# Splitting the projection's weight tiles by halves, with precedence for those of the values

## The chip, the cores and the metric

The kernel runs on one core of one Trainium2 chip. The metric is the device time of one execution in microseconds (us). The engines are named as in the profile: PE (TensorE, matrix products; PEld are its weight loads), ACT (ScalarE), DVE (VectorE), POOL (GpSimd) and SP (SyncE, which issues nearly all DMAs).

## The reference

The kernel computes one layer of a decoder for x of 1 x 1024 tokens x 1024, in float32. One input projection feeds two mixers side by side: a gated delta rule of 4 heads (mixer A, in chunks, a recurrence over the sequence) and a dilated window attention of 8 heads (mixer B). An output projection of both, and a gated MLP with a short convolution, follow.

```python
h = rmsnorm(x, norm1_w)
proj = h @ w_in                                   # q, k, v, z, beta, decay of A; q, k, v of B
qkv_a = silu(causal_dwconv(qkv_a, conv_qkv_w))    # A: convolution of 4 taps, then l2norm of q and k
o_a = rmsnorm(gated_delta_rule(qa, ka, va, g, beta), gdn_norm_w) * silu(z)
o_b = dilated_attention(qb, kb, vb)               # windows 128, 512, 2048 with strides 1, 4, 16
x = x + concatenate([o_a, o_b]) @ w_out
h = rmsnorm(x, norm2_w)
u = causal_dwconv(h @ w_up, ffn_conv_w)
x = x + (silu(gate) * up) @ w_down
return rmsnorm(x, final_norm_w)
```

## The kernel before, in words

**Products of split numbers.** [...] Each operand is split into a high part (a copy rounded to the type float32r) and a low part (the rest). `mm3` (line 199) multiplies high by high, high by low and low by high into one PSUM bank of 128 x 512. A weight tile of 128 x 1024 is loaded into a buffer wst (`raw_weight`, line 209), then split by `split` (line 205): ACT copies wst to whi, and DVE subtracts whi from wst into wlo. Each of wst, whi and wlo has a ring of two buffers. `weight` (line 214) does the split of one tile in two instructions, one on ACT and one on DVE, over all 1024 columns. `wk` (line 232) is `weight` for the output projection; `wk_by_halves` (line 222) does one tile there in two halves of 512 columns, with the urgent engines described below.

**The projections.** `dense` (line 491) goes through the columns in the order of DENSE (line 44): the last key tile, the values of mixer B in two groups (V 0 and V 1), q and v of mixer A by heads, q, k and v of mixer B by pairs ("a"), z. `take` (line 509) gives the tile that is due, splits the next one and loads the one after that. So a split is issued one tile ahead of its use.

- A V group (`values_by_token`, line 518) has four tokens' blocks as four banks of PSUM (two of the tag asc, two of ch) and four weight tiles j = 0 to 3 of in_wv. A tile holds two blocks of the contraction (kk = 0 and 1) of 512 columns each: for each block, each bank gets one mm3, 24 matrix products a tile. The first product of a bank in a group waits until the bank was emptied. After the group, ACT scales the four banks into vx (line 533, four evictions), and SP stores them by twos (line 535).
- Another tile (m-tile) holds eight blocks of 128 columns, and gives two banks of eight mm3 each, 48 products. Of its banks `scaled` (line 438) makes xr or aqkv on DVE. For keys, q and v of mixer A `conv_silu` (line 454) follows: a scaled copy on ACT, three steps kT<-xr,gcw,kT on DVE, then for keys a tanh (xr<-kT) on ACT and kT<-xr,kT on DVE.

**What else runs beside them.** `kprep` (line 595) prepares a head's keys: it loads rows of the decay into dec and, behind the key's last step, copies its ends to gel (DVE), takes eight exponentials dec<-dec,ngc and eg and ge (ACT), transposes the keys on PE and evicts them as ktok (ACT) with sums of squares sq; DVE makes bp, ke and um of the products of keys. Then come the triangular solve (DVE, some of it on small slices), the chain of the recurrent state over the chunks (ct, wke, r, w, vtok: short steps that alternate between PE, DVE and ACT), and the attention, whose scores sm are evicted with their maximum by DVE, exponentiated by ACT, transposed by PE and copied back as pt and pb by ACT and DVE.

**What sets the order.** PE's order is fixed when the kernel is built: streams of work (the generators above) run against a model of times, `Weave` (line 48), which asks for the `need` of tiles and gives each matrix product a place (`mm`, line 191, stamps it). The wrappers `Engine` (line 123) account ACT, DVE, POOL and SP in the model too, by a fixed part and a part per column. On ACT, DVE and SP the framework's scheduler orders the instructions afterwards by its own priorities: those of the plain wrappers `ac` and `ve` by their place in the program, those of the wrappers `ua` and `uv` (lines 153 and 154) 400 places (URGENT) earlier. Each engine works strictly in its order and waits there for what it needs.

A helper records all instructions under its own line: L141 and L143 in the profile are the ordinary and the urgent calls of the wrappers, L192 the products, L196 the transposes. Tiles are named by out<-in.

Of the kernel before, what the change touches and what calls it, by code (L numbers as in the profile page):

```python
# [7 lines left out]
F32 = mybir.dt.float32  # L8
F32R = mybir.dt.float32r
AF = mybir.ActivationFunctionType  # L10
OP = mybir.AluOpType
# [135 lines left out]
def hybrid_layer(tc, I, out):  # L147
    nc = tc.nc
    wv = Weave()
    ve = Engine(wv, nc.vector, "vector", 0.07, 0.00105)  # L150
    ac = Engine(wv, nc.scalar, "scalar", 0.12, 0.00085)

    uv = Engine(wv, nc.vector, "vector", 0.07, 0.00105, first=tc.high_priority)
    ua = Engine(wv, nc.scalar, "scalar", 0.12, 0.00085, first=tc.high_priority)
# [11 lines left out]
    def tile_(pool, shape, dt, name, tag, bufs):  # L166
        return wv.slot(pool.tile(list(shape), dt, name=name, tag=tag, bufs=bufs), tag, bufs)
# [3 lines left out]
    def A(name, tag, dt=F32, shape=(P, 1024)):  # L171
        if tag in TURNS:
            i = turns[tag] = turns.get(tag, -1) + 1
            tag = TURNS[tag][i % len(TURNS[tag])]
        return tile_(lp, shape, dt, name, tag, SLOTS[tag])
# [23 lines left out]
    def mm3(dst, lhs, rhs, first, last, **kw):  # L199
        us = 0.2135 * rhs[0].shape[-1] / 512  # L200
        mm(dst, lhs[0], rhs[0], us, first, False, **kw)
        mm(dst, lhs[0], rhs[1], us, False, False, **kw)
        mm(dst, lhs[1], rhs[0], us, False, last, **kw)

    def split(src, hi, lo):
        ac.activation(hi, src, AF.Copy)
        return ve.tensor_tensor(lo, src, hi.bitcast(F32), op=OP.subtract)

    def raw_weight(src, n=1024):
        st = tile_(wp, [P, n], F32, "wst", "wst", 2)  # L210
        sy.dma_start(st, src)
        return st

    def weight(src, n=1024, st=None):
        if st is None:
            st = raw_weight(src, n)
        hi = tile_(wp, [P, n], F32R, "whi", "whi", 2)
        lo = tile_(wp, [P, n], F32R, "wlo", "wlo", 2)
        split(st, hi, lo)
        return hi, lo  # L220

    def wk_by_halves(src):
# [34 lines left out]
    def bank(tag, name="ps"):  # L257
        return tile_(pp_, (P, 512), F32, name, tag, 2)
# [7 lines left out]
    def half(i):  # L266
        return slice(i * 512, i * 512 + 512)
# [170 lines left out]
    def scaled(pair, name, by_class=False, tag="ev", t=None, hs=(0, 1)):  # L438
        if t is None:
            t = A(name, tag)  # L440
        for h in hs:
            sl = half(h)
            if by_class:
                ve.tensor_tensor(t[:, sl].rearrange("p (n c u) -> p n u c", n=4, c=4),
                                        pair[h].rearrange("p (n u c) -> p n u c", n=4, c=4),
                                        rstdB[:, sl].rearrange("p (n u c) -> p n u c", n=4, c=4), op=OP.mult)
            else:
                ve.tensor_tensor(t[:, sl], pair[h], rstdB[:, sl], op=OP.mult)
        return t
# [4 lines left out]
    def conv_silu(xr, j, name, tag):  # L454
        y = A(name, tag)
        ac.activation(y, xr, AF.Copy, scale=gcw[:, j, 3:4])
        for d in (1, 2, 3):
            inst = ve.scalar_tensor_tensor(y[:, d:], xr[:, :S - d], gcw[:, j, 3 - d:4 - d], y[:, d:],
                                           op0=OP.mult, op1=OP.add)
            if j // 4 == 1 and d == 2 and klast:  # L460
                after(inst, klast[-1], "the keys before go first")
        if j // 4 != 1:
            ac.activation(y, y, AF.Silu)
            return y

        th = ac.activation(xr, y, AF.Tanh, scale=0.5)
        klast.append(ve.scalar_tensor_tensor(y, xr, 1.0, y, op0=OP.add, op1=OP.mult))
        kends[j - 4] = th, klast[-1]
        return y

    def silu2(xr, name):
        y = A(name, "ev")
        ac.activation(y, xr, AF.Tanh, scale=0.5)
        ve.scalar_tensor_tensor(y, y, 1.0, xr, op0=OP.add, op1=OP.mult)
        return y
# [8 lines left out]
    def first_keys():  # L484
        xr = [scaled(pst[2 * h:2 * h + 2], "xr", tag=("ev", "ev", "qa")[h]) for h in range(3)]
        for h in range(3):
            T["k", h] = conv_silu(xr[h], 4 + h, "kT", "kT*")
            wv.add(3, kprep(h))
            yield wv.need(T["k", h])

    def dense():

        yield from wv.until("first")
        yield from wv.until("norms")
        wv.add(2, first_keys())

        srcs, tiles = [], 0
        for col in DENSE:
            if col[0] == "V":
                srcs += [I["wv"][j] for j in range(4)]  # L500
            else:
                srcs.append(I["wi"][tiles])
                tiles += 1
        place = [0]
        raw = [raw_weight(srcs[0])]
        nxt = [weight(None, st=raw.pop())]
        raw.append(raw_weight(srcs[1]))

        def take():
            w = nxt.pop()  # L510
            i = place[0] = place[0] + 1
            if i < len(srcs):
                nxt.append(weight(None, st=raw.pop()))
            if i + 1 < len(srcs):
                raw.append(raw_weight(srcs[i + 1]))
            return w

        def values_by_token(g):

            banks = [bank(t) for t in ("asc", "asc", "ch", "ch")]  # L520
            for j in range(4):
                w = [t.rearrange("p (k m) -> p k m", k=2) for t in take()]
                for kk in range(2):
                    k = 2 * j + kk
                    for i, pt in enumerate(banks):
                        c = 4 * g + i
                        yield wv.need(pt, *w)
                        mm3(pt, [t[:, c * P:(c + 1) * P] for t in xs[k]], [t[:, kk, :] for t in w], k == 0, k == KT - 1)
            for i in range(0, 4, 2):
                vx = A("vx", "ev", shape=(P, 2, 512))  # L530
                for e in range(2):
                    c = 4 * g + i + e
                    ac.activation(vx[:, e, :], banks[i + e], AF.Copy, scale=rst[:, c:c + 1])
                c = 4 * g + i
                sy.dma_start(vpark[c * P:(c + 2) * P].rearrange("(e p) d -> p e d", e=2), vx)
            wv.done.add(("V", g))

        for i, col in enumerate(DENSE):
            kind, h = col[:2]
            if kind == "V":  # L540
                yield from values_by_token(h)
                continue
            if kind == "z":
                yield from wv.until(("o", h))
            w = [t.rearrange("p (k m) -> p k m", k=KT) for t in take()]
            pair = []
            for hh in range(2):
                pt = bank("hf")
                yield wv.need(pt, *w)
                for k in range(KT):  # L550
                    mm3(pt, [t[:, k, :] for t in w], [t[:, half(hh)] for t in xs[k]], k == 0, k == KT - 1)
                    yield 0.0

                pair.append(pt)
                if hh == 0:
                    xr = A("aqkv" if kind == "a" else "xr", "go" if kind == "k" else "ev")
                scaled(pair, "xr", kind == "a", t=xr, hs=(hh,))
            if kind == "k":
                T["k", h] = conv_silu(xr, 4 + h, "kT", "kT*")
                wv.add(3, kprep(h))  # L560
            elif kind == "q":
                q = conv_silu(xr, h, "qT", "qa")
                wv.add(4, qprep(h, q))
            elif kind == "v":
                v = conv_silu(xr, 8 + h, "vT", "qa")
                wv.add(4, vprep(h, v))
            elif kind == "z":
                og = gated[h] = A("og", "kT*")
                sy.dma_start(og, mixer[h])
                ve.tensor_tensor(og, og, silu2(xr, "zz"), op=OP.mult)  # L570
            else:
                sy.dma_start(apark[h, col[2]], xr)
                wv.done.add(col)
        wv.done.add("dense")
# [100 lines left out]
    def vprep(h, vT):  # L675
        yield from wv.until(("q", h))
        yield wv.need(vT, slack=SLACK)
        G[h]["vtok"] = yield from tokens(vT, A("vtok", ("dv", "dw")[h % 2]), G[h]["nk"])
        wv.done.add(("v", h))
# [952 lines left out]
```

## Time and profile before

| | us |
|---|---|
| median of three runs (lowest, highest) | 1207.66 (1207.51, 1208.27) |
| the profiled execution, its own time | 1208.24 |
| its span, first to last instruction | 1206.4 |
| PE busy | 1193.4 |
| DVE busy | 947.6 |
| ACT busy | 574.7 |
| POOL busy | 48.9 |

The clock granted to PE was 0.998 of full speed. A row of a timeline below has the start (us from the span's start), the length in us, engine, line, operation, out<-in, the shape of one instruction and xcount where neighbours of one kind are put together; in brackets stands the engine's idle time before the row and what ended it. Such a row's length for several instructions is that of all of them. Matmul ends are modelled, so the pitch of PE is read from starts. What an engine issues without being waited for costs nothing while PE is busy; a wait in PE's rows costs its length.

### The profile page before, as it was taken

The page shows a single profiled execution, that of the slowest core. Times are in us where ns is not written, and L with a number is a line of the kernel's source. Part 1 is how long each engine was busy: PE and PEld are TensorE (multiplying, and loading weights), DVE is VectorE, ACT ScalarE, POOL GpSimd, SP SyncE. Part 2 cuts the span into 40 slices and gives each one's busy share as a digit, 9 for nine tenths or more (in the row PEclk, how much of TensorE's full clock was granted, in tenths as well). Part 3 has the DMA queues.
Part 4 walks back from the last instruction along what each step waited for, and adds up shares of the span by engine and source line. Part 5 has one row for each costly group of instructions (what it writes and reads, how often), then busy time and mean ns, then how long its engine had stood idle before and what let it go on. Part 6 is the DMA issues. An engine that isn't in the chain of part 4 may idle for free.

```text
span 1206.4 us, 18292 instructions
## 1 busy us (share of the span) xinstructions
PE 1193.4 (99%) x7068; PEld 983.7 (82%) x7068; DVE 947.6 (79%) x1462; ACT 574.7 (48%) x1126; POOL 48.9 (4%) x46
## 2 busy tenths in 40 slices
PE   9999999999999999999999999999999999999997
PEld 7878888888777778888888888888888888888886
DVE  7684965666477686767988988889898889999875
ACT  7384344356344452655545445444454454444441
POOL 0211010003100000000000000000000000000000
PEclk9999999999999999999999999999999999999999
DMA  7425253435624213544213132231322298546513
GB/s 233 109 74 160 82 128 112 146 123 151 227 98 128 82 36 107 175 136 150 75 66 105 54 104 85 72 105 53 105 69 89 93 367 307 180 161 226 165 54 140
DMA packets 85798, 154.80 MB, mean 128 GB/s; under 512 B 21168, under 2 KB 36304, under 8 KB 85712
## 3 DMA queue, kind: packets, MB, share of 16 engines
q1 hardware_dynamic: 85136, 153.12, 39.5%
q8 instruction: 55, 0.90, 0.3%
q10 hardware_dynamic: 576, 0.52, 0.1%
q14 instruction: 31, 0.25, 0.1%
HBM read 117.68 MB, written 35.93 MB: 127 GB/s over the span
## 4 chain that ended last, share of the span: by engine, by line
PE 94%; DVE 3%; issue 1%; ACT 1%; POOLq 0%; POOL 0%; DVEq 0%; ACTq 0%
PE ps L192 43%; PE pa L192 20%; PE dw L192 17%; PE pc L192 10%; PE ps L196 3%; DVE kT L141 1%; PE warm L192 1%; DVE wlo L141 1%; DVE xr L141 0%; DVE x1h L141 0%; PE pd L192 0%; DVE sm L143 0%; DVE qT L141 0%; ACT dec L141 0%; ACT sq L143 0%
## 5 line engine op out<-in xcount | busy, mean ns | idle before, releaser
L192 PE MATMUL dw<-pr 128*128 128x512 f32 (+1 forms) x984 | 211.3, 376 | 0.0
L192 PEld LDWEIGHTS dw<-pr 128*128 128x128 f32 x984 | 176.6, 188 | 33.6
L192 PE MATMUL ps<-xhi,whi 128*128 128x512 f32 x384 | 158.1, 412 | 0.0
L192 PE MATMUL ps<-xhi,wlo 128*128 128x512 f32 x384 | 150.3, 391 | 0.0
L192 PE MATMUL ps<-xlo,whi 128*128 128x512 f32 x384 | 149.9, 390 | 0.0
L192 PE MATMUL pa<-T,pair 128*128 128x512 f32 x528 | 127.1, 389 | 0.0
L192 PEld LDWEIGHTS pa<-T,pair 128*128 128x128 f32 x528 | 99.0, 188 | 20.6
L192 PEld LDWEIGHTS ps<-xhi,wlo 128*128 128x128 f32 x384 | 72.1, 188 | 15.7
L192 PEld LDWEIGHTS ps<-xhi,whi 128*128 128x128 f32 x384 | 72.2, 188 | 14.8 <-issue 1.4
L192 PEld LDWEIGHTS ps<-xlo,whi 128*128 128x128 f32 x384 | 72.4, 189 | 12.0
L141 ACT ACTIVATE u<-pa 128x512 f32<-128x512 f32 x44 | 26.3, 598 | 107.3 <-PE pa L192 107.3
L141 ACT ACTIVATE whi<-wst 128x1024 fp32r<-128x1024 f32 (+2 forms) x41 | 41.9, 1022 | 74.0 <-PE ps L192 64.7
L141 DVE SCALAR_TENSOR_TENSOR y<-xu,fcw,y 128x1023 f32<-128x1023 f32 (+1 forms) x44 | 56.4, 1281 | 22.1 <-ACT y L141 22.0
L143 ACT ACTIVATE sm<-sm,mx 128x128 f32<-128x128 f32 (+7 forms) x64 | 35.4, 555 | 60.0 <-DVE mx L143 60.0
L192 PE MATMUL pa<-B,A 128*128 128x512 f32 x264 | 63.4, 389 | 0.0
L192 PE MATMUL pc<-T,S 128*128 128x512 f32 x264 | 63.4, 389 | 0.0
L192 PE MATMUL pa<-T,S 128*128 128x512 f32 x264 | 63.4, 389 | 0.0
L192 PE MATMUL pc<-B,pair 128*128 128x512 f32 x264 | 63.4, 389 | 0.0
L141 DVE TENSOR_TENSOR wst<-wst 128x512 f32<-128x512 f32 x88 | 60.6, 688 | 0.9
L192 PE MATMUL ps<-B,pair 128*128 128x512 f32 x252 | 60.5, 389 | 0.0
L141 DVE TENSOR_TENSOR wlo<-wst,whi 128x1024 fp32r<-128x1024 f32 (+2 forms) x41 | 48.2, 1175 | 14.9 <-ACT whi L141 14.9
L192 PEld LDWEIGHTS pa<-B,A 128*128 128x128 f32 x264 | 49.5, 188 | 10.3
(244 smaller groups left out, 2349.2 us busy)
## 6 DMA issues: line engine op xcount, KB each, us to landing
wst<-in_wu SPq DMA_DIRECT2D x44, 512.0 KB, 3.7
wd<-in_wd SPq DMA_DIRECT2D x44, 512.0 KB, 4.4
upark<-y SPq DMA_DIRECT2D x22, 512.0 KB, 3.8
wst<-in_wi SPq DMA_DIRECT2D x21, 512.0 KB, 3.7
r<-upark SPq DMA_DIRECT2D x11, 512.0 KB, 7.4
r<-upark SPq DMA_DIRECT2D x22, 256.0 KB, 6.8
wa<-in_wd SPq DMA_DIRECT2D x22, 256.0 KB, 3.1
wst<-in_wv SPq DMA_DIRECT2D x8, 512.0 KB, 3.6
```

What stands on the lines that cost most here:

```text
L141: return getattr(eng, op)(*a, **kw)
L143: return getattr(eng, op)(*a, **kw)
L192: tc.stamp_issue_order_token(nc.tensor.matmul(dst, lhs, rhs, start=start, stop=stop, **kw).ins, TOKEN)
L196: tc.stamp_issue_order_token(nc.tensor.transpose(dst, src, ident if idt is None else idt).ins, TOKEN)
```

## The change

`weight` splits a tile in two halves of 512 columns, each with one copy on ACT and one subtraction on DVE; where `urgent` is given, these go through the wrappers `ua` and `uv`. `take` gives `urgent` for the tiles that are split on its first eight calls: the eight tiles of in_wv. All tiles of 128 x 1024 that go through `weight` are split by halves: 21 of in_wi, 8 of in_wv and 7 of in_wo, 36 tiles, so ACT and DVE have 36 instructions more each. The matrix products, the loads, the buffers and the numbers computed stay the same.

```diff
-    def weight(src, n=1024, st=None):
+    def weight(src, n=1024, st=None, urgent=False):
         if st is None:
             st = raw_weight(src, n)
         hi = tile_(wp, [P, n], F32R, "whi", "whi", 2)
         lo = tile_(wp, [P, n], F32R, "wlo", "wlo", 2)
-        split(st, hi, lo)
+        for sl in (half(0), half(1)):
+            (ua if urgent else ac).activation(hi[:, sl], st[:, sl], AF.Copy)
+            (uv if urgent else ve).tensor_tensor(lo[:, sl], st[:, sl], hi[:, sl].bitcast(F32), op=OP.subtract)
         return hi, lo
...
             w = nxt.pop()
             i = place[0] = place[0] + 1
             if i < len(srcs):
-                nxt.append(weight(None, st=raw.pop()))
+                nxt.append(weight(None, st=raw.pop(), urgent=1 <= i <= 8))
             if i + 1 < len(srcs):
                 raw.append(raw_weight(srcs[i + 1]))
             return w
```

## The prediction

> **What bounds the kernel now.** I read the page first: the span, the busy shares and the chain that ended last.
>
> ```profile
> span 1206.4 us, 18292 instructions
> PE 1193.4 (99%) x7068; PEld 983.7 (82%) x7068; DVE 947.6 (79%) x1462; ACT 574.7 (48%) x1126; POOL 48.9 (4%) x46
> PE 94%; DVE 3%; issue 1%; ACT 1%; POOLq 0%; POOL 0%; DVEq 0%; ACTq 0%
> ```
>
> The matmul engine is busy in 1193.4 of 1206.4 us. No edit of splits takes a matmul away, so all that can be won is PE's idle time, 13.0 us in the whole span, and all that can be lost is new idle time on PE. The waits of PE by releaser say how much of it belongs to weights:
>
> ```profile
> PE ps L192 <- DVE wlo L141: 1.1, 1, 1.1
> PE ps L192 <- ACT whi L141: 0.4, 1, 0.4
> ```
>
> One wait each. The timeline of PE shows where they are, the third tile (j=2) of the first value group:
>
> ```profile
> 73.41 0.39 PE L192 MATMUL ps<-whi,xlo 128*128 128x512 f32 x1
> 74.20 0.51 PE L192 MATMUL ps<-whi,xhi 128*128 128x512 f32 x1 [0.41 <-ACT whi L141]
> 75.83 0.50 PE L192 MATMUL ps<-wlo,xhi 128*128 128x512 f32 x1 [1.12 <-DVE wlo L141]
> 76.16 0.39 PE L192 MATMUL ps<-whi,xlo 128*128 128x512 f32 x1
> 76.39 0.40 PE L192 MATMUL ps<-whi,xhi 128*128 128x512 f32 x1
> ```
>
> Unhindered products start 0.23 us apart (76.16 to 76.39). Here they start 0.79 and 1.63 apart: 0.56 + 1.40 = 1.96 us is lost to this tile, and this is the whole prize. The timelines of ACT and DVE show why it is late:
>
> ```profile
> 70.54 2.47 ACT L141 ACTIVATE dec<-dec,ngc 128x128 f32<-128x128 f32 x8
> 72.98 0.22 ACT L141 ACTIVATE ge<-gel 128x8 f32<-128x8 f32 x1
> 73.08 1.07 ACT L141 ACTIVATE whi<-wst 128x1024 fp32r<-128x1024 f32 x1
> 70.71 3.92 DVE L141 SCALAR_TENSOR_TENSOR kT<-xr,gcw,kT 128x1023 f32<-128x1023 f32 x3 [0.23 <-ACT kT L141]
> 74.55 1.22 DVE L141 TENSOR_TENSOR wlo<-wst,whi 128x1024 fp32r<-128x1024 f32 x1
> ```
>
> ACT comes to the high part only after eight exponentials of the decay, DVE to the low part only after three steps of a convolution. PE waits for DVE last.
>
> **The change part by part.** *The halves' price.* One tile of the kernel is already split by halves (its rows are L143 here), so the price is in the trace (ACT's timeline, and the tile view with least, median and most):
>
> ```profile
> 495.79 1.15 ACT L143 ACTIVATE whi<-wst 128x512 fp32r<-128x512 f32 x2 [5.41 <-PE ps L192]
> L143 DVE TENSOR_TENSOR wlo<-wst,whi x2: 685/686/686, 496.6 to 497.8; 128x512 fp32r<-128x512 f32 x2
> ```
>
> Two halves on ACT take 1.15 us against 1.07 for the whole tile at 73.08: 0.08 more. On DVE 2 x 0.686 - 1.22 (74.55) = 0.15 more, less the overlap of neighbours (the whole split of 74.55 follows a group that ends at 74.63, 0.08 later): 0.07. With 36 tiles of 128x1024 that is 36 x 0.08 = 2.9 us on ACT and 36 x 0.07 = 2.5 us on DVE. Neither is on the chain; a weight tile is taken one tile ahead, and a tile is 48 products (11 us) long in the m-tiles, 24 (5.5 us) in the values' tiles. I cost this at nothing. It is covered by PE; without that cover it would be 2.5 to 2.9 us.
>
> *The stalled tile.* In the built order of the changed kernel the precedence moves this tile's high halves past one instruction only, ge (0.1 us of issue, 72.98 to 73.08), and its low halves not at all: they still stand behind the three kT steps. So only the halving helps. DVE starts half a at 74.55 and ends it 0.69 later, at 75.24, instead of 75.77. PE gains about 0.5 us (floor 0, if the kT steps end later; ceiling 1.96, had the precedence put the split first).
>
> *The other value tiles, and a new wait.* The precedence does move the splits of the tiles behind. Three moves matter:
>
> ```profile
> 78.14 1.23 DVE L141 SCALAR_TENSOR_TENSOR kT<-xr,kT 128x1024 f32<-128x1024 f32 x1
> 79.48 2.45 ACT L141 ACTIVATE dec<-dec,ngc 128x128 f32<-128x128 f32 x8 [0.43 <-DVE gel L141]
> 80.55 1.12 DVE L141 SCALAR_TENSOR_TENSOR um<-ps,bp,dec 128x128 f32<-128x128 f32 x4
> 81.59 1.22 DVE L141 TENSOR_TENSOR wlo<-wst,whi 128x1024 fp32r<-128x1024 f32 x1
> 83.25 1.06 ACT L141 ACTIVATE whi<-wst 128x1024 fp32r<-128x1024 f32 x1 [1.21 <-issue]
> ```
>
> First, tile j=3: both low halves, and four um in between, now stand ahead of the key's kT at 78.14. That is 2 x 0.61 (half of 1.22) + 1.04 (80.55 to 81.59) = 2.26 us later for kT, for gel behind it, and so for dec, which waits for gel. ACT has 1.21 us of idle time ahead of 83.25 to take up; 2.26 - 1.21 = 1.05 us of lag stays on ACT's queue.
>
> Second, ACT at the change from the first value group to the second. The group's four banks are emptied by four evictions vx, and the next group's first product in a bank waits for its eviction:
>
> ```profile
> 88.23 1.33 ACT L141 ACTIVATE vx<-ps,rst 128x512 f32<-128x512 f32 x2
> 89.37 2.51 ACT L141 ACTIVATE dec<-dec,ngc 128x128 f32<-128x128 f32 x8
> 91.72 0.26 ACT L141 ACTIVATE eg<-gend 128x8 f32<-128x8 f32 x1
> 91.91 1.32 ACT L141 ACTIVATE vx<-ps,rst 128x512 f32<-128x512 f32 x2
> 92.71 0.50 PE L192 MATMUL ps<-whi,xhi 128*128 128x512 f32 x1
> 93.50 0.39 PE L192 MATMUL ps<-whi,xhi 128*128 128x512 f32 x1
> ```
>
> PE's third and fourth banks start at 92.71 and 93.50; the last vx ends at 93.23, 0.27 ahead of the fourth, so this place has no slack now. In the changed order ACT runs vx vx vx, five dec, the two urgent halves of the second group's tile, three dec, eg, ge, and only then the fourth vx. From the first vx: 3 x 0.57 + 8 x 0.294 + 1.06 + 0.19 = 5.31 us to the start of the last, 0.66 for it and 0.27 to PE: 6.24. With the first vx at 88.23 the fourth bank starts at 94.47, with 1.05 of lag at 95.52. That is **+1.0 to +2.0 us** for PE; I take 2.0, since every row of the chain that carries the lag is there. PE gets to this place earlier by the 0.5 us won at 75 and waits, so the gain is inside this number and not counted again. What is queued behind the fourth vx (ktok, and its squares) is later by as much and PE with it. The price is an absolute date of PE, and nothing later on PE is idle enough to give it back.
>
> Third, the DMA queue of SP: the second vpark store (behind the fourth vx) now stands behind an in_wv load and a store; the values are fetched again only in the attention stage, over 200 us on: nothing.
>
> *The other projection tiles, without precedence.* Their halves stand where the scheduler's dates put them. The windows view shows where PE has idle time (columns: length, then busy of PE, PEld, DVE, ACT, POOL, clock, DMA share, GB/s), 1.52 us at 60 to 80 and 0.73 at 260 to 280; below it one wait of PE in the recurrent chain and two rows of the output projection:
>
> ```profile
> 60.00:80.00 20.00, 18.48 (x92) 14.98 (x91) 15.47 (x26) 18.20 (x65) 3.28 (x2) 1.00 0.18 54
> 260.00:280.00 20.00, 19.27 (x156) 18.45 (x155) 17.17 (x60) 13.46 (x58) 0.30 (x1) 1.00 0.35 111
> ```
>
> ```profile
> 259.29 0.49 PE L192 MATMUL ps<-ct,kT 128*128 128x128 f32 x2 [0.45 <-DVE ct L143]
> ...
> 476.61 0.40 PE L192 MATMUL ps<-olo,whi 128*128 128x512 f32 x1
> 477.03 0.50 PE L192 MATMUL ps<-ohi,wlo 128*128 128x512 f32 x1
> ```
>
> The recurrent chain (from about 200 to 300 us) is bound by short steps across PE, ACT and DVE, as the wait for ct at 259.29 shows; one low half moves ahead of such a step there (wke) and holds it by up to its 0.6: I take +0.2 (bounds -0.45, the wait gone, and +0.8). In the output projection the product of the low part starts 0.42 after its neighbour instead of 0.23; a half would be there in time: -0.2 (0 to -0.2).
>
> In the attention stage two places get worse. At the first scores,
>
> ```profile
> 317.54 1.28 ACT L143 ACT_TABLE_LOAD   x1
> 325.04 0.40 ACT L143 ACTIVATE sm<-sm,mx 128x128 f32<-128x128 f32 x1 [6.22 <-DVE mx L143]
> 326.52 0.34 PE L196 MATMUL ps<-ident,sm 64*128 64x64 f32 x4
> ```
>
> the table load for the exponentials ran 7 us ahead. Now it and the exponentials stand behind two high halves, which wait for PE's last product of an older tile. Six products of PE move ahead of the scores (1.4 us, no cost in themselves), so the transposes of sm want to start at 327.9; the halves run from about 325.4, the load to 327.8, the two first exponentials to 328.6, and the transposes wait: +0.8 (0 to 1.4). At the fourth pair,
>
> ```profile
> 352.13 0.36 DVE L143 COPY pt<-ps 128x256 f32<-128x256 f32 x1
> 353.13 0.47 DVE L143 COPY pb<-ps 128x128 f32<-128x128 f32 x2
> 353.52 1.07 DVE L141 TENSOR_TENSOR aqkv<-ps,rstdB 128x512 f32<-128x512 f32 x1
> 355.11 1.09 PE L192 MATMUL ps<-pt,vn 128*64 128x128 f32 x16
> ```
>
> DVE now runs aqkv and one low half ahead of the copies and the other half between them: 0.93 + 2 x 0.6 = 2.1 later, so the last copy ends at 355.7 where PE wants it by about 354.8: +1.0 (0 to 1.5). Of another gap of this size at a later pair I count -0.25, an estimate from the 0.2 above. Sum of the stage +1.55.
>
> **Sum.** 2.0 + 0.2 + 1.55 - 0.2 = +3.55 us. The profiled execution took 1208.24 us with a span of 1206.4; the runs shown have a median of 1207.66, 0.6 lower. On the span this gives 1210.0, on the profiled execution 1211.8, on the median **1211.2 us**.
>
> [...]
>
> **The rivals.**
>
> *Only the stall shrinks (not slower).* The halves end PE's wait earlier, and the fourth eviction is in time after all, since its place in the queue costs only if ACT really runs through 88 to 94 without a pause. For it: ACT idled 1.21 us ahead of 83.25, so that it has some room. Against it: none of ACT's rows from 88.23 to 91.91 shows idle time before it. Time: 1207.66 - 0.5 = 1207.2, at the ceiling 1205.7. It decides if the fourth vx ends by 93.2.
>
> *The eviction alone.* The attention places are covered, because the order that I read there moves the halves by less than the slack. Time: 1207.66 + 1.0 to 2.0 = 1208.7 to 1209.7.
>
> *The halves cost more.* The chain at 260 and the two attention places each take their upper bound: 2.0 + 0.8 + 1.4 + 1.5 = 5.7, 1213.4.
>
> *Full relief.* Precedence removes all 1.96 us, and other weight waits that the view puts down to other engines go as well (0.25 and 0.2): 1207.66 - 2.4 = 1205.2. Against it: DVE's place in the queue did not change for the stalled tile.
>
> **How the numbers follow.** The chances: forecast (1210.1 to 1212.3) 0.54, eviction alone 0.24, only the stall 0.12, more cost 0.06, full relief 0.04. The lower bounds of the terms sum to 1.0 - 0.45 - 0.25 - 0.2 = +0.1, the stall's gain alone ends at 1207.2, the upper case at 1213.4: the range 1207.0 to 1213.4 takes in the first four. About 0.2% (2.4 us) is what a measurement of this kernel can tell from no change: faster means under 1205.24, slower over 1210.08. Faster: 0.04. Within: 0.12 + 0.24 = 0.36, as the forecast's range ends above that bound. Slower: 0.54 + 0.06 = 0.60.
>
> **What would show it.** In the changed profile, the wait on wlo near 75 us should be about 0.6 instead of 1.12; a new wait of about 2 us on ACT vx should stand near 93 to 95 us, with the urgent halves (rows of L143) just ahead of the fourth vx on ACT. New waits of about 0.8 and 1.0 us should stand near 328 and 355 us (plus the shift). ACT and DVE should be busy 3 to 5 us longer, the clock 1.00 in all windows. The prediction is wrong if PE starts the fourth bank before 94 us, or if the attention waits are not there.

## The result, and the profile after

The changed kernel took 1213.49 us (median of five runs, 1211.65 to 1213.65), the kernel before 1208.24 beside it (1207.51 to 1209.36): ratio 1.0037, 95% interval 1.0026 to 1.0049. That is slower by more than 0.2%. On the 1207.66 us from which the prediction counts, the ratio gives 1212.1 (1210.8 to 1213.6), against 1211.2 predicted; the five runs' own median lies 0.1 us above the predicted range. The sign and most of the mechanism were right; one term was missing.

The profiled execution is one of 1213.65 us. The page's head and the chain that ended last:

```profile
span 1211.9 us, 18364 instructions
PE 1194.7 (99%) x7068; PEld 983.9 (81%) x7068; DVE 950.7 (78%) x1498; ACT 578.3 (48%) x1162; POOL 49.5 (4%) x46
PE 92%; DVE 3%; ACT 2%; issue 1%; DMA 1%; SPq 0%; POOLq 0%; POOL 0%; DVEq 0%; ACTq 0%
```

ACT and DVE, with 36 instructions more each, are busy for 3.6 and 3.1 us more. The span grew by 5.5, and PE's busy time only by 1.3: the rest is idle time of PE and of the end. The waits of PE (us in total, times, longest) show where to look:

```profile
PE ps L192 <- ACT vx L141: 2.2, 1, 2.2
PE ps L192 <- DVE wlo L143: 1.1, 1, 1.1
...
PE ps L192 <- DVE xlo L141: 0.8, 1, 0.8
PE ps L192 <- DVE pb L143: 0.6, 1, 0.6
...
PE ps L196 <- ACT sm L143: 0.4, 1, 0.4
```

The wait on vx is new and the largest; those on pb and sm are new too; that on whi is gone. The wait on xlo (at 12 us) is new in this profile as well, but it costs nothing: PE had come there 1.2 us sooner than in the kernel before, and at 12.5 us the two are level. PE's timeline at the stalled tile and at the group's change:

```profile
73.49 0.40 PE L192 MATMUL ps<-whi,xlo 128*128 128x512 f32 x1
73.85 0.50 PE L192 MATMUL ps<-whi,xhi 128*128 128x512 f32 x1
75.47 0.50 PE L192 MATMUL ps<-wlo,xhi 128*128 128x512 f32 x1 [1.11 <-DVE wlo L143]
...
92.65 0.40 PE L192 MATMUL ps<-whi,xlo 128*128 128x512 f32 x1
95.22 0.50 PE L192 MATMUL ps<-whi,xhi 128*128 128x512 f32 x1 [2.17 <-ACT vx L141]
...
97.16 0.63 PE L192 MATMUL ps<-wlo,xhi 128*128 128x512 f32 x1
97.58 0.63 PE L192 MATMUL ps<-whi,xlo 128*128 128x512 f32 x1
```

At the stalled tile, starts are 0.36 and 1.62 us apart where unhindered ones are 0.23: 1.52 us are lost instead of 1.96, a gain of 0.44. At the group's change the fourth bank starts at 95.22 instead of 93.50. And then the rows show what the prediction did not have: from 97.16 on the products start 0.42 us apart instead of 0.23. The windows of 1 us (busy of PE, PEld, DVE, ACT, POOL, then the granted clock, DMA share, GB/s), four of the changed kernel and then one of the kernel before, say why:

```profile
96.00:97.00 1.00, 1.00 (x6) 0.98 (x5) 0.00 (x0) 0.03 (x1) 0.00 (x0) 0.58 0.63 49
97.00:98.00 1.00, 1.00 (x3) 0.72 (x3) 0.00 (x0) 1.00 (x6) 0.00 (x0) 0.50 0.88 363
98.00:99.00 1.00, 1.00 (x4) 0.79 (x3) 0.00 (x0) 0.60 (x5) 0.00 (x0) 0.50 1.08 410
99.00:100.00 1.00, 1.00 (x7) 0.80 (x6) 0.00 (x0) 0.00 (x0) 0.00 (x0) 0.71 0.35 131
```

```profile
140.00:141.00 1.00, 1.00 (x6) 0.76 (x5) 1.00 (x3) 1.00 (x2) 0.00 (x0) 1.00 1.03 418
```

The granted clock falls to half for 3.4 us, beginning 0.9 us after PE has resumed; below this is called the dip. The kernel before shows 1.00 at 97 to 98 us, and it also shows 1.00 at 140 us, where its DMAs are as busy and move as much (a share of 1.03 and 418 GB/s, against 1.08 and 410). So DMA traffic of this size made no dip there.

Why the fourth eviction is late stands in ACT's timeline:

```profile
81.66 2.46 ACT L141 ACTIVATE dec<-dec,ngc 128x128 f32<-128x128 f32 x8 [2.23 <-DVE gel L141]
...
89.16 1.88 ACT L141 ACTIVATE vx<-ps,rst 128x512 f32<-128x512 f32 x3
90.87 1.62 ACT L141 ACTIVATE dec<-dec,ngc 128x128 f32<-128x128 f32 x5
92.34 1.19 ACT L143 ACTIVATE whi<-wst 128x512 fp32r<-128x512 f32 x2
93.38 1.02 ACT L141 ACTIVATE dec<-dec,ngc 128x128 f32<-128x128 f32 x3
...
94.45 0.72 ACT L141 ACTIVATE vx<-ps,rst 128x512 f32<-128x512 f32 x1
```

No row from 89.16 on has idle time ahead of it: ACT runs through, with the urgent halves (L143) in the queue ahead of the fourth vx, which ends at 95.17, 0.05 ahead of PE. The first row carries the lag: dec starts 2.18 us later than before (79.48).

Where the time went, by the starts of the same numbered matrix products (the attention by the products ahead of and behind it, since the two kernels order those within it differently):

| place | predicted, us | profiled executions, us |
|---|---|---|
| the stalled tile | -0.5, swallowed by the next | -0.46, swallowed by the next |
| fourth bank, against before | +2.0 | +1.72 |
| clock at half, 96 to 99 us | 0 | +1.67 |
| recurrent chain | +0.2 | -0.1 |
| attention | +1.55 | +1.6 |
| output projection | -0.2 | -0.3 |
| MLP, and the landing of the output after PE's end | 0 | +0.24 and +0.6 |

The sum is 5.4; the spans differ by 5.5. The last row's two parts are of single executions and of no place that the change touches.

### The profile page after: what moved, and what is told of

Same layout as the page of the kernel before. It is cut to its first block, busy times and chain, and to the rows that moved or that the text cites. A ratio compares the mean times of both kernels' runs of the same rounds, so it can differ in the third digit from the quotient of the medians.

```text
span 1211.9 us, 18364 instructions
## 1 busy us (share of the span) xinstructions
PE 1194.7 (99%) x7068; PEld 983.9 (81%) x7068; DVE 950.7 (78%) x1498; ACT 578.3 (48%) x1162; POOL 49.5 (4%) x46
## 4 chain that ended last, share of the span: by engine, by line
PE 92%; DVE 3%; ACT 2%; issue 1%; DMA 1%; SPq 0%; POOLq 0%; POOL 0%; DVEq 0%; ACTq 0%
PE ps L192 43%; PE pa L192 20%; PE dw L192 17%; PE pc L192 10%; PE ps L196 3%; DVE kT L141 1%; DMA xt<-in_xT 1%; ACT sm L143 0%; ACT dec L141 0%; DVE xr L141 0%; DVE wlo L141 0%; ACT whi L141 0%; DVE x1h L141 0%; PE pd L192 0%; DVE qT L141 0%
## 5 line engine op out<-in xcount | busy, mean ns | idle before, releaser
L141 ACT ACTIVATE whi<-wst 128x512 fp32r<-128x512 f32 (+2 forms) x61 | 35.8, 633 | 69.1 <-PE ps L192 63.3
L143 ACT ACTIVATE sm<-sm,mx 128x128 f32<-128x128 f32 (+7 forms) x64 | 35.4, 555 | 52.2 <-DVE mx L143 52.2
L141 ACT ACTIVATE pr<-r 128x1024 fp32r<-128x1024 f32 (+1 forms) x44 | 36.3, 839 | 45.3 <-PE dw L192 29.9
L192 PEld LDWEIGHTS pc<-T,S 128*128 128x128 f32 x264 | 49.6, 188 | 10.3
```

The lines of the kernel that those rows point to most:

```text
L141: return getattr(eng, op)(*a, **kw)
L143: return getattr(eng, op)(*a, **kw)
L192: tc.stamp_issue_order_token(nc.tensor.matmul(dst, lhs, rhs, start=start, stop=stop, **kw).ins, TOKEN)
```

## The experiments

Each kernel ran beside the kernel before on the same chip, 5 to 11 runs of it against 20 to 33 of before. My theory at the start: the precedence costs, not the halves, by the place of the fourth vx in ACT's queue; the attention's loss comes with the halves, by the order that is planned from them; the slow clock follows from the long wait. The rivals: the added instructions cost by themselves, everywhere; the halves of the value tiles are enough to make the wait; the slow pitch belongs to the changed order and not to the wait. A letter in an expectation names a theory as it stood for that run: A, A1 and A2 are versions of mine, the others are rivals.

**All tiles by halves, no precedence.**

```diff
-                nxt.append(weight(None, st=raw.pop(), urgent=1 <= i <= 8))
+                nxt.append(weight(None, st=raw.pop(), urgent=False))
```

> All 36 tiles by halves, none with precedence; the four evictions keep their place ahead of the halves, as before the change. Theory A (the loss is the fourth eviction held behind the precedence, 2.1 us, and the halved clock right after it, 1.7 us; the other projection tiles cost a net 1.2 us, nearly all in the attention stage): no wait for vx near 93 us, clock 1.00 at 95 to 100 us, about 0.9 us over the kernel before (1.2 less about 0.3 won at the stalled tile). Theory B (36 more instructions on ACT and on DVE cost the time wherever they stand): about 4 us over the kernel before, as the changed kernel.

Measured 1208.82 us against 1208.06, ratio 1.0006 (0.9997 to 1.0015). PE's waits in its profile:

```profile
PE ps L192 <- DVE pb L143: 0.6, 1, 0.6
PE ps L192 <- DVE wlo L141: 0.5, 1, 0.5
...
PE ps L196 <- ACT sm L143: 0.4, 1, 0.4
```

There is no wait on vx, and the clock is 1.00 at 96 to 100 us; the waits on pb and sm are as in the changed kernel. So the added instructions by themselves cost nothing that these runs can tell, the attention's loss belongs to the halves, and 4.1 to 4.5 us of the change's 4.8 to 5.3 (differences of medians, with the repetition below) come with the precedence of the halves.

**Precedence, but whole tiles.**

```diff
-        for sl in (half(0), half(1)):
+        for sl in (slice(0, 1024),):
```

> Whole tiles again, with the precedence for the eight tiles of the values. Only the fourth eviction stands behind a whole high part (0.97 us of ACT), and no decay exponentials change place. Theory A: a wait for vx of about 0.9 us near 93 us, too short for the clock to fall, attention stage as before, the wait for the stalled tile as before: +0.9 us. Theory B: 0 over the kernel before, since no instruction is added. A third reading (the clock falls for any wait there): +2.5 us.

Measured 1208.5, ratio 1.0004 (0.9995 to 1.0013). PE's waits:

```profile
PE ps L192 <- DVE wlo L143: 1.1, 1, 1.1
...
PE ps L192 <- ACT vx L141: 0.6, 1, 0.6
...
PE ps L192 <- ACT whi L143: 0.4, 1, 0.4
```

The stalled tile is as in the kernel before: the precedence alone does nothing for it. A shorter wait on vx is there (0.6 instead of the 0.9 us expected), the attention's are not. The medians differ by 0.44 us, half of what was expected. So neither the halves alone (0.76) nor the precedence alone costs much; it takes both.

**The changed kernel, with precedence for vx too.**

```diff
-                    ac.activation(vx[:, e, :], banks[i + e], AF.Copy, scale=rst[:, c:c + 1])
+                    ua.activation(vx[:, e, :], banks[i + e], AF.Copy, scale=rst[:, c:c + 1])
```

> The changed kernel with the evictions vx under the same precedence: the fourth one stands ahead of the two halves and of three of the eight decay exponentials. Theory A: it ends at about 93.0 instead of 95.2 us, PE waits under 0.3 us there, and the clock stays at 1.00: 3.5 us under the changed kernel's profiled run, 1.0 to 1.3 us over the kernel before. Theory B: no change against the changed kernel. If the clock dip had a cause of its own: 2 us under the changed kernel, with the clock still down at 96 to 99 us.

Measured 1209.43, ratio 1.0011 (1.0002 to 1.0020). The wait on vx is gone, and so is the slow clock; 3.5 to 3.9 us of the loss go with them. So the fourth vx's place is the cause of the wait; the next kernel, which keeps that place, keeps the wait.

**Halves and precedence for the value tiles only.**

```diff
-        for sl in (half(0), half(1)):
+        for sl in (half(0), half(1)) if urgent else (slice(0, 1024),):
```

> Halves with precedence for the eight tiles of the values, all other tiles whole as before. Theory A: the same wait of 2.2 us near 93 to 95 us and the same fall of the clock behind it, attention stage as before: +3.4 us over the kernel before in runs with the fall, +1.7 in runs without it. Theory B: a quarter of the changed kernel's loss (8 of 36 tiles), +1 us.

Measured 1210.28, ratio 1.0019 (1.0010 to 1.0028). Its row of PE at the fourth bank, and its windows behind it:

```profile
94.01 0.50 PE L192 MATMUL ps<-whi,xhi 128*128 128x512 f32 x1 [2.13 <-ACT vx L141]
```

```profile
95.00:96.00 1.00, 1.00 (x6) 0.99 (x5) 0.00 (x0) 0.11 (x1) 0.00 (x0) 0.50 0.85 217
96.00:97.00 1.00, 1.00 (x4) 0.73 (x3) 0.00 (x0) 1.00 (x6) 0.00 (x0) 0.50 0.96 373
97.00:98.00 1.00, 1.00 (x4) 0.81 (x3) 0.00 (x0) 0.52 (x5) 0.00 (x0) 0.50 0.81 305
```

The same wait and the same slow clock, and no loss in the attention. The wait and the attention's loss are separate causes. The time was not as expected: +3.4 us was expected of a run with the dip, and the profiled one has the dip at +2.2, as its fourth bank starts at 94.01 and not at 95.22. Of these 1.2 us, about 0.8 may come from steps of DVE at 52 us that the change does not touch, an estimate from the pair of profiles in the last section (0.84): the wait on wlo is 0.5 here, as in the shorter of that pair, and 1.1 in the longer. The eleven runs (1209.02 to 1211.83) form no two groups.

**Halves with precedence for the first value group's tiles only**, the others by plain halves.

```diff
-                nxt.append(weight(None, st=raw.pop(), urgent=1 <= i <= 8))
+                nxt.append(weight(None, st=raw.pop(), urgent=1 <= i <= 4))
```

> All tiles by halves, with precedence only for the tiles of the first value group. No urgent half can then stand ahead of the fourth vx, but the key's dec keep their lag of about 1 us. Theory A (two causes at the eviction, the lag of dec by about 1 us and the urgent halves by about 1.1 us): a wait on vx of 0.8 to 1.2 us, clock mostly 1.00, the attention steps as with all halves (+2.6, of which 1.1 to 1.4 are given back): +1.0 to +2.2 us. Theory B (the urgent halves of the second group are the whole cause): no wait on vx, +0.6 us as with halves and no precedence.

Measured 1210.62, ratio 1.0019 (1.0010 to 1.0028). ACT's timeline:

```profile
88.07 1.89 ACT L141 ACTIVATE vx<-ps,rst 128x512 f32<-128x512 f32 x3
89.78 2.49 ACT L141 ACTIVATE dec<-dec,ngc 128x128 f32<-128x128 f32 x8
...
92.33 0.72 ACT L141 ACTIVATE vx<-ps,rst 128x512 f32<-128x512 f32 x1
92.89 1.19 ACT L141 ACTIVATE whi<-wst 128x512 fp32r<-128x512 f32 x2
```

The halves of the second group now stand behind the fourth vx, and PE waits 1.1 us for it, not 2.2. So the wait has the two parts of the prediction, each about half: the lag that the first group's urgent halves put on dec, and the second group's halves in the queue. Its clock is 1.00 from 93 to 101 us. The median is 2.35 us over that of the kernel before, 0.15 above what was expected.

**Halves only for the two tiles split last before the first scores** (calls 21 and 22 of `take`), all others whole and no precedence.

```diff
-        for sl in (half(0), half(1)):
+        for sl in (half(0), half(1)) if halves else (slice(0, 1024),):
...
-                nxt.append(weight(None, st=raw.pop(), urgent=1 <= i <= 8))
+                nxt.append(weight(None, st=raw.pop(), halves=21 <= i <= 22))
```

> Of all tiles only the two ahead of the first scores of the attention (the 21st and 22nd that take splits) go by halves, without precedence; the tile that is split at the scores themselves is whole. Theory A1 (the loss in the attention is one of order: the planner accounts two halves otherwise than a whole tile, puts six products ahead of the scores, and from there on ACT's table load and DVE's copies stand behind splits): the same steps as with all tiles by halves, +1.3 us near 328 and +1.3 near 355 us, and 1.1 us given back by 395 us; +1.5 us over the kernel before. Theory A2 (the halves that stand in front of the waiting work cost it their own length): nothing, within 0.2 us of the kernel before.

Measured 1208.68, ratio 1.0009 (1.0000 to 1.0017). Its ACT ahead of the first scores:

```profile
326.37 1.06 ACT L141 ACTIVATE whi<-wst 128x1024 fp32r<-128x1024 f32 x1 [5.75 <-PE ps L192]
327.45 1.28 ACT L143 ACT_TABLE_LOAD   x1
328.74 0.40 ACT L143 ACTIVATE sm<-sm,mx 128x128 f32<-128x128 f32 x1
```

The split at this place is a whole one, and the table load stands behind it all the same, where the kernel before has it 7 us ahead. PE loses 1.35 us net from the products ahead of the attention to those behind it (1.6 in the changed kernel), though no tile in that stage is halved. So no half costs there by its own length: two halves far ahead suffice to plan PE otherwise, and the new plan takes a weight tile ahead of the scores. In the model each half has a fixed part of its own; that this is what tips the plan is read from the code and was not tested. The time alone would not show the loss: the median is 0.5 us over that of the kernel before, where 1.5 was expected, and the profiled execution is one of the longer ones (1210.50).

**Halves only for the next two tiles** (calls 23 and 24), with the same edit and `halves=i in (23, 24)`.

> The counterpart: only the two tiles that are split at the first scores and at the fourth pair (the 23rd and 24th) go by halves. The order of everything else stays that of the kernel before. Theory A1: no step near 328 and 355 us, within 0.2 us of the kernel before. Theory A2: both steps, +2.6 us there.

Measured 1208.51, ratio 1.0007 (0.9999 to 1.0016); PE's waits on sm and pb are absent and no step shows in the attention. With the run before, this leaves the plan made ahead of the scores as the cause. It rests on the two profiles and not on the times, whose medians differ by 0.2 us.

**The wait alone.** In the kernel before, one or two copies of 128x512 into vx, overwritten at once, stand on ACT ahead of the fourth vx of the first group; no weight tile is halved that was not.

```diff
+                    for _ in range(2 if (g, i, e) == (0, 2, 1) else 0):
+                        after(nc.scalar.activation(vx[:, 1, :], rstdB[:, :512], AF.Copy), third)
+                    third = ac.activation(vx[:, e, :], banks[i + e], AF.Copy, scale=rst[:, c:c + 1])
-                    ac.activation(vx[:, e, :], banks[i + e], AF.Copy, scale=rst[:, c:c + 1])
```

> The kernel before with whole tiles, and one copy of 128x512 more on ACT ahead of the fourth eviction, whose result is overwritten; the split of the next tile slips in front too. The fourth eviction is late by 0.57 + 0.97 us, PE waits about 1.4 us near 93 us. Theory A (the fall of the clock follows from the length of PE's wait, between 0.8 us without it and 2.2 us with it): open on which side 1.4 us lies; +1.4 us over the kernel before if the clock stays, +3 us if it falls. If the fall came from the halves or from the DMAs of that moment, it is not there.

One copy: 1209.38, ratio 1.0012 (1.0003 to 1.0021), a wait of 1.1 us where 1.4 was expected (the whole split slips in front too), and no dip in the profile. Eight runs lie from 1208.12 to 1209.89; three of 1210.58 to 1211.25 have a mean clock of 0.996 instead of 0.997 to 0.998.

> The kernel before, no tile by halves but the one that already was, with two overwritten copies of 128x512 on ACT ahead of the fourth vx: the wait alone, without what the change does elsewhere. Both theories: a wait of PE on vx of 1.7 to 2.1 us near 93 us, no step at 328 and 355 us. Theory A (a wait of this length at this place brings the clock down in part of the executions): slow pitch of 0.43 for about 3 us from about 95 us in part of the runs; a median of +2.0 to +3.7 us, runs 1.2 to 1.8 us apart. Theory B (the slow pitch comes from the changed order, not from the wait): +1.8 to +2.1 us, clock 1.00 from 94 to 100 us, runs no further apart than those of before.

Two copies: 1210.18, ratio 1.0022 (1.0013 to 1.0032). Six runs lie from 1209.33 to 1210.22, four from 1212.15 to 1213.05, the six at a mean clock of 0.997 to 0.998, the four at 0.995 to 0.997. The profiled execution is of the lower group:

```profile
94.43 0.50 PE L192 MATMUL ps<-whi,xhi 128*128 128x512 f32 x1 [1.74 <-ACT vx L141]
```

```profile
96.00:97.00 1.00, 1.00 (x6) 0.80 (x5) 0.00 (x0) 1.00 (x6) 0.00 (x0) 1.00 1.09 266
```

A wait without any of the change's halves divides the runs into two groups, 2.3 us apart by their medians. That the upper four have the dip is inferred from their clock and time, for the execution with a profile has none. The expectations don't decide it: the median (+1.9 us) and the clock of the profile fit the rival, that the dip belongs to the changed order, and the distance of the groups fits mine. Against the rival stands a profile of another kernel, that with the tiles of calls 21 and 22 halved: it has a dip near 76 us, where its order is that of the kernel before (last section).

**The changed kernel again**, beside the last two.

> The changed kernel once more, beside the two below. Both theories: +3.5 to +5.3 us against before. Theory A (the clock halves for about 3 us after the 2.2-us wait in some executions, at a price of about 1.7 us): the runs fall into two groups about 1.8 us apart, the upper one with a granted clock lower by 0.001. Theory B (the slow pitch belongs to the changed order, in every execution): one group near +4.5 to +5.

Measured 1213.11 against 1208.27, ratio 1.0035 (1.0022 to 1.0048): one run of 1210.70 at a clock of 0.997, four of 1213.05 to 1213.69 at 0.996. With the first five that makes three runs up to 1211.76 and seven from 1213.05 on, and nothing between. The profile, of the run of 1213.11, has the wait (2.1 us) and a clock of 0.50 from 96 to 98 us. So both profiled runs of the upper group show the dip; no run of the lower group has a profile.

**The split placed by hand.** Only the first tile, the stalled one (call 3), the last four and the output projection's are halved. `after(x, y)` puts x behind y: the stalled tile's high halves stand ahead of its eight dec, its low halves behind the first kT step. vx has precedence.

```diff
+        if urgent:
+            after(convs[2], lo_i)
+            for inst in decs[8 + 0:16]:
+                after(inst, hi_i)
...
+                nxt.append(weight(None, st=raw.pop(), urgent=i == 3, halves=i == 3 or i >= 25))
...
+                    ua.activation(vx[:, e, :], banks[i + e], AF.Copy, scale=rst[:, c:c + 1])
```

> The stalled tile's halves put by hand where the precedence did not bring them (high part ahead of the eight decay exponentials, low part behind the first of three kT steps), the evictions vx with precedence, halves else only for the z tiles and the output projection. Theory A: no weight wait near 74 us (1.5 to 2.0 us won, or 1.1 where the key steps come early), under 0.7 us of wait for the fourth eviction, no step in the attention, 0.2 won in the output projection: 1.2 to 2.2 us under the kernel before.

Measured 1206.74 (1205.79 to 1207.61) against 1208.17, ratio 0.9988 (0.9979 to 0.9997): faster than both kernels, though against the kernel before by 0.2% at most. DVE and PE at the tile that was stalled:

```profile
70.97 1.28 DVE L141 SCALAR_TENSOR_TENSOR kT<-xr,gcw,kT 128x1023 f32<-128x1023 f32 x1 [0.22 <-ACT kT L141]
72.17 1.28 DVE L141 TENSOR_TENSOR wlo<-wst,whi 128x512 fp32r<-128x512 f32 x2
73.38 2.59 DVE L141 SCALAR_TENSOR_TENSOR kT<-xr,gcw,kT 128x1022 f32<-128x1022 f32 x2
```

```profile
73.01 0.39 PE L192 MATMUL ps<-whi,xlo 128*128 128x512 f32 x1
73.24 0.39 PE L192 MATMUL ps<-whi,xhi 128*128 128x512 f32 x1
```

All of the prize of 1.96 us is won here (1.9 by PE's starts). Then 0.77 is lost by 88 us to a wait on sq (0.5), as the key is later by the two low halves put ahead of its steps.

## Why the prediction was right, and where it was not

- **The bound, the prize and the stalled tile.** Right. The prize, the idle time that could be won at the stalled tile, was 1.96 us (the last experiment wins it), and halving without a better place wins 0.46, against 0.5. The row named for it was wrong: I expected the wait on wlo to fall to 0.6, but it stays at 1.11. What went is the wait on whi, whose first half is there sooner; PE comes to the low part 0.35 us earlier and waits for it until 75.47 instead of 75.83.
- **The fourth eviction.** Right, and the largest term: the fourth vx starts 5.29 us after the first, 5.31 was worked out; the lag of the first vx is 0.93 (89.16 to 88.23), 1.05 was; the bank starts at 95.22, 95.52 was. Vx with precedence removes it, and the first group's halves alone give half of it. The rival in which only the stall shrinks, because ACT has room, falls.
- **The step that failed: "the clock 1.00 in all windows".** I priced PE's wait at its length. In both profiled executions it costs more, since PE runs at half clock for 3.4 us behind it (+1.67 in the first). The ten runs' groups, 1.8 us apart by their medians, suggest that seven had the dip. By the terms, a run without it is -0.46 + 2.2 (the swing at the fourth bank) + 1.5 - 0.3 = +2.9, and the three lower runs, 1210.70, 1211.65 and 1211.76, lie 2.4 to 3.5 above before's medians. The predicted +3.55 is near these, and the median is that of a run with the dip. That the ratio's 1212.1 still lies within the range is in part luck: the upper end stood there for a chain and an attention that cost more, and neither did.
- **The attention.** The size is right, 1.55 against 1.6, and so are its parts by PE's starts: 0.76 at the first scores (0.8 was predicted), 1.3 at the fourth pair (1.0), -0.45 later (-0.25). The waits in PE's rows are shorter than the 0.8 and 1.0 that were named as signs, 0.4 on sm and 0.6 on pb. The cause was read partly wrong: I let the halves' own position and length delay the table load and the copies, but two tiles halved far ahead shift the plan, and whole splits in the same places cost as much (1.35).
- **The halves' price.** Costed at nothing under PE's cover: no run speaks against it. All tiles by halves without precedence cost 0.76 us in the median, which -0.46 + 1.5 - 0.3 accounts for.
- **The chain.** It loses 0.3 us at 260 us and has won it back by 310, so it comes out even (the table's -0.1 includes the way there); +0.2 was predicted, and its bounds hold.

Open: what decides whether 1.5 to 1.8 us of idle time bring a dip (the last section has cases of both kinds), how much of the groups is the dip and how much the steps of DVE at 52 us, and where the 0.6 us between the plain halves and vx with precedence lie (their intervals overlap). A kernel with all tiles by halves and PE's plan of before was not tried.

## What to carry to other kernels

A precedence for an instruction is a demotion for all that it passes: look at each place where it passes an eviction that frees a PSUM bank, and price that in dates of the matmul engine (here 1.72 us at the fourth bank). If a model of times plans the order, a change in its costs alone can move work far from the edit; halve only where the plan stays. And look at the clock behind a long wait of the matmul engine before pricing it by its length alone: in the profiles here single waits of up to 1.1 us brought no dip, one of 1.7 us none, a pair of 0.4 and 1.1 us one in three profiles, and all three waits of more than 2 us did.

## What the runs showed of the hardware

**Half the clock behind a short idle.** After waits of 2.1 to 2.2 us (three profiles) the granted clock went to 0.50, and products started 0.42 us apart instead of 0.23. It also went down behind a shorter stall: in the kernel with the tiles of calls 21 and 22 halved, after the waits of 0.4 and 1.1 us at the stalled tile, which this kernel has as the one before. The windows below are cut at the edges of the dip and of the stretch of the same length ahead of it, first of the changed kernel, then of this one (the clock is the third figure from the end of a row):

```profile
92.75:96.16 3.41, 1.24 (x7) 0.76 (x6) 1.29 (x2) 2.42 (x8) 0.00 (x0) 1.00 0.65 70
96.16:99.57 3.41, 3.41 (x13) 2.72 (x12) 0.00 (x0) 1.63 (x9) 0.00 (x0) 0.50 0.78 273
```

```profile
72.96:76.37 3.41, 1.90 (x8) 1.03 (x7) 2.47 (x3) 3.41 (x17) 0.00 (x0) 1.00 0.00 0
76.38:79.79 3.41, 3.41 (x13) 2.95 (x12) 2.62 (x7) 2.98 (x9) 1.64 (x1) 0.50 0.50 154
```

The next row is of the kernel with two copies, a stretch of the same length that holds its whole wait of 1.74 us; no dip is behind it, the clock is 1.00 up to 101 us:

```profile
91.96:95.37 3.41, 1.67 (x8) 1.01 (x8) 1.23 (x1) 2.39 (x4) 0.00 (x0) 1.00 0.27 45
```

Four profiles have a dip, and each dip lasts 3.4 us, 3.413 by the clock's record in the trace of the changed kernel. It begins 0.35 to 0.94 us after PE has resumed, so not at a fixed distance. In all four the stretch of 3.41 us just ahead of the dip holds PE's whole stall: 1.5 to 2.2 us of it are idle. So much idle time didn't always bring a dip: the last row above has 1.74 us, more than the 1.51 of the row at 72.96, and no dip follows.

The clock falls to 0.50 once more behind the last product of an execution, at 1205.49 us in the changed kernel and at 1201.50 in the kernel before. In the clock's records of these two traces each stretch at one clock, up to that fall, is a whole multiple of 3.4133 us: 92.16 (27 times), 3.413 and 1105.92 (324 times) in the changed kernel, 1194.67 (350 times) in the kernel before. Counted back in such lengths from 1201.50, one of them ends at 75.10 us in the kernel before, in the middle of its stall, with 0.80 and 0.72 us of idle time in the two beside it (3.41 less PE's busy time in the windows at 71.69 and 75.10), and there is no dip. That the place of a stall among such lengths decides on the dip, and so makes a part of the difference between executions of one kernel, is a guess of mine and was not shown. The kernel before may have a dip too in its longest runs; none of those has a profile.

**DVE beside POOL.** The same four steps of the convolution on DVE took 7.60 us in the profile of the changed kernel and 6.76 in that of the kernel with vx in precedence too, while POOL selected in dec. The timelines of DVE and POOL, first of the changed kernel, then of the other:

```profile
52.04 7.60 DVE L141 SCALAR_TENSOR_TENSOR kT<-xr,gcw,kT 128x1023 f32<-128x1023 f32 x4
...
55.17 3.39 POOL L141 TENSOR_SCALAR_AFFINE_SELECT dec<-dec 128x1024 f32<-128x1024 f32 x2 [0.66 <-DMA dec<-gdram]
```

```profile
51.91 6.76 DVE L141 SCALAR_TENSOR_TENSOR kT<-xr,gcw,kT 128x1023 f32<-128x1023 f32 x4
...
53.63 6.00 POOL L141 TENSOR_SCALAR_AFFINE_SELECT dec<-dec 128x1024 f32<-128x1024 f32 x3 [1.27 <-DMA dec<-gdram]
```

Three such steps take 3.92 us beside no selection (70.71 in the kernel before), so four would take about 5.2, an estimate; beside the selections they take 1.5 or 2.4 us more. The size does not follow the edits: the changed kernel and the one with vx in precedence too differ only in the precedence of vx, whose first row is at 89.16 us, and the kernel before has 7.63 us there, the one with precedence and whole tiles 7.62. Where DVE is the quicker, POOL's selections are the longer: 2.0 us each in the last row of the second pair, 1.7 in that of the first. The 0.84 between the two profiles moves the stalled tile (-0.46 or -1.27 us against before, with the same halves there), and is more than the halving is worth: single profiles can't be compared at that place without this row, and the times of single runs may differ by it too. No run shows whether one of the two engines holds up the other.
